# Weight loads for gating tied to evictions, and the last normalised rows written to other tiles

## The chip, the core and the metric

The kernel runs on one core of a Trainium2 chip. Its engines work side by side, each through its own queue in program order: PE (TensorE, matrix products into PSUM banks), DVE (VectorE) and ACT (ScalarE), which read PSUM and SBUF, POOL (GpSimd), which also issues DMAs, and SP (SyncE), which here only issues DMAs. Semaphores order them. The metric is the device time of one execution in microseconds (us); the median of several runs is compared.

## The reference

One layer of a diffusion backbone over 1024 latent tokens and 256 context tokens, model width 1024, everything in float32. Cut to what matters here:

```python
h_lat = rms_norm(x, norm1_g) * (1 + sc1) + sh1
p = h_lat @ w_in                      # 7 column blocks of 512: retention q,k,v,gate; attention q,k,v
y = concat(retention(...), diff_attention(...)) @ w_out
x = x + g1 * y                        # g1: one number for each of the 1024 columns
h2 = rms_norm(x, norm2_g) * (1 + sc2) + sh2
x = x + g2 * conv_ffn(h2, w_up, conv_w, conv_b, w_down)
return rms_norm(x, final_g)
```

The projection, the retention (chunks of 128 tokens, two directions), the attention, the output projection and the feed-forward part follow one another; every product of `rms_norm` needs a row's whole sum of squares first.

## The kernel before

**Products in halves.** Float32 operands are split into a high and a low part (`whi` on ACT, `wlo` on DVE) and each product is three passes on PE: high by high, high by low, low by high (lines 133 to 135). The two large products, the output projection and the feed-forward part, are built by a scheme of seven block products instead of eight, so that sums and differences of blocks are formed first (`sums_in_place`, `combined`, `t1_d`, `w13_d`, `w2_d`).

**The projection.** `stream_block(b)` loads one column block of `w_in` in four slices of 512 KB (`raw`, line 195, on SP) and splits each into `whi` and `wlo` (lines 202 and 203). There are two buffers for `raw` and five for the split slices, so a fifth slice, slice 0 of the next block, is split early and the others when PE has finished with the old block. `natural` then makes eight tiles of 128 tokens, `pn`, each of 24 matmuls; `store_to` evicts a tile on ACT (`st`, line 469) and stores it. At each of the eight steps of a tile `tick()` advances two side jobs by rates. In the block of the retention's gates (number 3) and the one of the attention's values (number 6) these are:

- `side`: with block 3 `states_before`, the backward states of the retention. It loads keys and values in pairs (`kvgb`, line 237, on SP, three pairs ahead), multiplies on PE (`pub`, line 363) and updates the state on DVE (`Sb`, lines 248 and 250). With block 6 it is `outputs`: 32 steps of scores, outputs, square root on POOL (line 119), gating of a head and transposing (`pc`, `po`, `ss`, `o`, `y`, `pyt`).
- `along`: `weight_blocks`, which multiplies `w_out` by g1. It loads the 1024 gate numbers (`g1`, 512 KB over 128 partitions, on SP) and, for c = 0 to 3, two blocks of `w_out` of 512 KB on POOL's DMA queue (`load`, line 423), multiplies their halves by g1 on DVE (`gated`, line 427), forms a difference (`t1`) and a combination on DVE, and stores three results on POOL's queue (`kept`, line 430). Its rate is 0.3 steps a tick, beginning at a count of −5. The loads themselves wait only for their buffers (an older tile's last reader); nothing ties them to a place in the projection.

**The output projection's end.** `out_product` makes a 512-wide half of 128 rows; `to_x1` adds it to `x1[t]` on DVE (line 1347). `squared` stores that half of `x1[t]` to DRAM for the last residual (`x1d`, line 1285, on SP) and sums its squares on ACT. `norm2` adds the two sums, takes the power −1/2 on POOL (line 1297) and scales the whole row block in place (line 1298). Rows 0 to 3 come first; rows 7, 4, 5, 6 are the last, in this order. In between stand `turned0` (rows 0 to 3 transposed and split into B11 and B21), the splitting of the first three weight blocks of the feed-forward part (`early`), and the sums of two further blocks, one on DVE and one on POOL (`sums_in_place`, lines 1329 to 1331; POOL goes on with `combined`, line 1512). Behind that PE begins the feed-forward products (`chain`, `second`) with `turned1` beside them: rows 4 to 7 transposed (`pt`, line 1304), combined on DVE (line 1454) and split. The products `fifth`, `third` and the later ones of `chain` follow.

**What sets the order.** Instructions are written in the order of the Python code, a scheduler orders each engine's queue by its own estimates, and `tc.issue_after` or `tc.add_manual_dep` ties one instruction to another. A dependency of class NoSync fixes the order alone; one of class Sync is a wait. Here the order of `weight_blocks` among its neighbours follows from the two numbers above.

Of the kernel before, what the change touches and what calls it, by code (L numbers as in the profile page):

```python
# [8 lines left out]
F32 = mybir.dt.float32  # L9
# [3 lines left out]
ALU = mybir.AluOpType  # L13
# [4 lines left out]
P = 128  # L18
D = 1024
# [40 lines left out]

TAIL = 2
GAP = 128
PREP_RATE, PREP_DUE = 0.3, -5.0
SPARE = (16, 4)
MOD_TICKS = 7
FIRST_LOADS = (22, 23, 25, 26, 28, 30)
# [10 lines left out]
def kernel(  # L77
# [16 lines left out]
    nc = tc.nc  # L94
# [17 lines left out]
    mhalf = kp.tile([P, 32], F32, name="mhalf")  # L112
# [27 lines left out]
    g1_d = dr.tile([P, D], F32, name="g1d")  # L140
# [19 lines left out]
    with ExitStack() as p1:  # L160
# [26 lines left out]
        marks = {}  # L187
# [227 lines left out]
        def weight_blocks():  # L415
            shared = rp.tile([P, 2, 2, 512], F32, name="g1", tag="rtab")
            g1 = shared[:, 0]
            nc.sync.dma_start(out=g1.rearrange("p n e -> p (n e)"), in_=g1_d)
            blocks = {}

            def load(c, i):
                t = blocks[c, i] = shared[:, 1] if c % 2 > i else er.tile([P, 2, 512], F32, name=f"w{i}x", tag="xhl")
                nc.gpsimd.dma_start(out=t, in_=w_out[:, :, 4 * i + c, :].rearrange("n p e -> p n e"))

            def gated(t, half):
                with tc.issue_after(marks["last"]):
                    nc.vector.tensor_tensor(out=t[:, half, :], in0=t[:, half, :], in1=g1[:, half, :], op=ALU.mult)

            def kept(dst, o):
                nc.gpsimd.dma_start(out=dst, in_=o)  # L430

            load(0, 0)
            load(0, 1)
            load(1, 0)
            for c in range(4):
                wa, wb = blocks[c, 0], blocks.get((c, 1))
                for half in range(2):
                    yield
                    gated(wa, half)
                    if c and not half:  # L440
                        load(c, 1)
                        wb = blocks[c, 1]
                yield
                t1 = er.tile([P, 512], F32, name="t1", tag=("xa", "xb")[c % 2])
                with tc.issue_after(marks["last"]):
                    nc.vector.tensor_tensor(out=t1, in0=wa[:, 1, :], in1=wa[:, 0, :], op=ALU.subtract)
                kept(t1_d[c], t1)
                for half in range(2):
                    yield
                    gated(wb, half)  # L450
                kept(w2_d[c], wb)
                yield
                nc.vector.tensor_tensor(out=wa[:, 1, :], in0=wb[:, 1, :], in1=wa[:, 1, :], op=ALU.subtract)
                kept(w13_d[c], wa)
                if c < 2:
                    load(c + 2, 0)

        def natural(wget, lhs, tiles, finish):
            for t in tiles:
# [6 lines left out]
        def store_to(dst, func=AF.Copy, scale=1.0, c0=0, center=False):  # L466
            def fin(t, pt):
                st = ev.tile([P, 4, P], F32, name="st", bufs=3)
                nc.scalar.activation(st.rearrange("p h e -> p (h e)"), pt, func, scale=scale)
                if center:  # L470
                    mu = ev.tile([P, 32], F32, name="mu")[:, 0:4]
                    nc.vector.tensor_reduce(out=mu, in_=st, axis=AX.X, op=ALU.add)
                    nc.vector.tensor_scalar(out=mu, in0=mu, scalar1=1.0 / P, scalar2=None, op0=ALU.mult)
                    nc.vector.tensor_tensor(out=st, in0=st, in1=mu.unsqueeze(2).to_broadcast([P, 4, P]), op=ALU.subtract)
                nc.sync.dma_start(out=dst(c0 + t), in_=st)

            return fin
# [815 lines left out]
    def norm2(t):  # L1293
        squared(t, right if t < 4 else left)
        rs = sm2[:, t : t + 1]
        nc.vector.tensor_tensor(out=rs, in0=rs, in1=sm2[:, NT + t : NT + t + 1], op=ALU.add)
        power = nc.gpsimd.tensor_tensor(out=rs, in0=rs, in1=mhalf[:, :1], op=ALU.pow).ins
        nc.vector.tensor_scalar(out=x1[t], in0=x1[t], scalar1=rs, scalar2=None, op0=ALU.mult)
        return power

    def turned(hf, d, raw, on_act):
        pt = turn_tile[0]()
# [30 lines left out]
    with ExitStack() as p3:  # L1333
# [10 lines left out]
                tick()  # L1344

        def to_x1(t, cols, ps):
            nc.vector.tensor_tensor(out=x1[t][:, cols], in0=ps, in1=x1[t][:, cols], op=ALU.add)

        def split_into(o, src):
            nc.scalar.copy(o[:, 0, :], src)  # L1350
# [74 lines left out]
            to_x1(4 + r, right, chain[r])  # L1425
            squared(4 + r, right)
        pre = [raw_load("wra" if j < 2 else "wrb", w_up[j]) for j in range(NPRE)]
        early = [[split_op(a[:, c : c + 4, :]) for c in (0, 4)] for a in pre]
        raws = [up_load(j) for j in range(NSUM)]
        sums_in_place(nc.vector, *raws[0])  # L1430
        for r in (3, 0, 1, 2):
            out_product(chain[r], r, y22o, t4o, False)
            to_x1(4 + r, left, chain[r])
            scaled = norm2(4 + r)
        with tc.issue_after(scaled):
            sums_in_place(nc.gpsimd, *raws[1])
        beside(iter(()), 0.0)
    x1lS.close()

# [79 lines left out]
        return dict(p1=a1, p2=a2, p3=b1, p4=b2, p5=s1, p6=s2, p7=s3)  # L1519

    chain, second, first, fifth, third = {}, {}, {}, {}, {}
    with tc.issue_after(scaled):
        ops = [combined(j) for j in range(NSUM)]
    split_ahead = []
    beside(turned1(), 0.5, -2.5)
    for j in range(NPRE):
# [522 lines left out]
```

## Time and profile before

| | |
|---|---|
| median of 3 runs | 1389.15 us (1388.04 to 1390.73) |
| the profiled execution | 1389.36 us |
| its span, first to last instruction | 1387.6 us |
| mean granted clock of TensorE | 0.996 |
| busy: PE, DVE, ACT, POOL | 1357.2, 1055.5, 758.5, 385.2 us |
| projection blocks 3 and 6 (latent tokens) | some 269 to 397 us of the span |
| last rows of the output projection | some 728 to 748 us |

All times in the profile are us from the first instruction. A row of the timeline has start, duration, engine, line, operation, written tile `<-` read tiles, shapes and a count; in square brackets stands how long the engine had been idle before it and what ended that. A row of waits has the waiting instruction, the one waited for, the sum, the number of waits and the longest. A row of stretches has the stretch, its length, the busy time of PE, PE's weight loads, DVE, ACT and POOL with the numbers of instructions, then the granted clock, the share of the 16 DMA engines that was busy, and GB/s. `SPq` rows are DMA issues. Line numbers are those of the kernel before.

### The profile page before, as it was taken

The numbers are of one execution on the slowest core, as the hardware profiler recorded it, in microseconds if no ns is written. First come the engines' busy times: TensorE is split into PE (matmuls) and PEld (weight loads), VectorE is DVE, ScalarE is ACT, GpSimd is POOL, SyncE is SP. The second block draws the span as 40 slices with busy tenths as digits, with TensorE's granted clock in tenths as the row PEclk, the third lists the DMA queues.
The fourth block names the chain that finished last, engine by engine and source line by source line (L and its number), as shares of the span: only waits on it lengthen the run. The fifth ranks groups of instructions, "written<-read, shape, count | busy, mean of one in ns | idle before, by whom it ended". The sixth has DMA issues, their size and how long they took to land.

```text
span 1387.6 us, 19752 instructions
## 1 busy us (share of the span) xinstructions
PE 1357.2 (98%) x6980; PEld 1138.4 (82%) x6980; DVE 1055.5 (76%) x1543; ACT 758.5 (55%) x1462; POOL 385.2 (28%) x422
## 2 busy tenths in 40 slices
PE   7999999999999999999999999999999999999997
PEld 5788888877888789999887888888888888788886
DVE  4967766644566888888878999888778877898756
ACT  5536534312457789988546645555544555455533
POOL 1310001611545354542102244222333220043003
PEclk9999999999999999999999999999999999999999
DMA  9467887799669595340714223332323326953324
GB/s 379 157 201 255 293 271 245 255 329 323 213 225 248 129 254 119 64 86 1 273 69 129 91 107 115 114 114 93 112 104 110 114 76 221 373 190 109 125 99 152
DMA packets 111499, 240.60 MB, mean 173 GB/s; under 512 B 10212, under 2 KB 42468, under 8 KB 109992
## 3 DMA queue, kind: packets, MB, share of 16 engines
q1 hardware_dynamic: 100360, 206.30, 43.7%
q0 software_dynamic: 10896, 32.77, 9.5%
q8 instruction: 55, 0.90, 0.3%
q14 instruction: 44, 0.36, 0.1%
q10 hardware_dynamic: 144, 0.26, 0.1%
HBM read 170.62 MB, written 68.42 MB: 172 GB/s over the span
## 4 chain that ended last, share of the span: by engine, by line
PE 61%; DMA 3%; DVE 1%; POOL 1%; issue 0%; ACT 0%; SPq 0%; POOLq 0%; DVEq 0%; ACTq 0%
PE chain L133 6%; PE chain L134 6%; PE chain L135 6%; PE pA L959 5%; PE pv L991 5%; PE c L135 4%; PE c L134 4%; PE c L133 4%; PE third L133 3%; PE third L135 3%; PE third L134 3%; PE pt L979 2%; DMA W<-w_down 2%; PE second L135 1%; PE second L134 1%; PE second L133 1%
## 5 line engine op out<-in xcount | busy, mean ns | idle before, releaser
L133 PE MATMUL pl<-hT,whi 128*128 128x512 f32 x256 | 107.6, 420 | 0.0
L133 PE MATMUL chain<-T,whi 128*128 128x512 f32 x264 | 102.8, 390 | 0.0
L134 PE MATMUL chain<-T,whi 128*128 128x512 f32 x264 | 102.7, 389 | 0.0
L135 PE MATMUL chain<-T,wlo 128*128 128x512 f32 x264 | 102.7, 389 | 0.0
L962 DVE TENSOR_REDUCE mt<-pA 128x1 f32<-128x1280 f32 x64 | 95.1, 1489 | 9.1 <-PE pA L959 8.4
L135 PE MATMUL pl<-hT,wlo 128*128 128x512 f32 x256 | 100.5, 392 | 0.0
L134 PE MATMUL pl<-hT,whi 128*128 128x512 f32 x256 | 100.2, 391 | 0.0
L1515 POOL TENSOR_TENSOR cmb<-wrb 128x512 f32<-128x512 f32 x20 | 30.5, 1523 | 235.1 <-DMA wrb<-w_up 171.3
L135 PE MATMUL c<-whi,ghl 128*128 128x512 f32 x232 | 90.4, 389 | 1.1 <-DVE ghl L1810 1.1
L134 PE MATMUL c<-wlo,ghl 128*128 128x512 f32 x232 | 90.3, 389 | 0.0
L133 PE MATMUL c<-whi,ghl 128*128 128x512 f32 x232 | 90.3, 389 | 0.0
L959 PE MATMUL pA<-ks,qhl 128*128 128x512 f32 (+1 forms) x384 | 89.6, 368 | 0.0
L966 ACT ACTIVATE p<-pA,mt 128x1280 f32<-128x1280 f32 x64 | 85.4, 1334 | 4.4 <-DVE mt L962 4.0
L133 PE MATMUL pn<-whi,hT 128*128 128x512 f32 x192 | 85.7, 446 | 1.2 <-ACT whi L202 1.2
L503 ACT ACTIVATE xb<-pl 32x512 f32<-32x512 f32 (+1 forms) x88 | 51.9, 590 | 60.9 <-PE pl L135 41.3
L1252 ACT CAST whi<-cmb 128x512 fp32r<-128x512 f32 x62 | 38.4, 622 | 77.1 <-PE chain L134 61.9
L135 PE MATMUL pn<-whi,hT 128*128 128x512 f32 x192 | 76.6, 400 | 1.0 <-POOL hT L668 1.0
L959 PEld LDWEIGHTS pA<-ks,qhl 128*128 128x128 f32 x384 | 68.1, 190 | 11.4
L134 PE MATMUL pn<-wlo,hT 128*128 128x512 f32 x192 | 76.2, 397 | 0.8 <-DVE wlo L203 0.8
L991 PE MATMUL pv<-va,aT 128*128 128x128 f32 x640 | 76.8, 275 | 0.0
L991 PEld LDWEIGHTS pv<-va,aT 128*128 128x128 f32 x640 | 74.0, 192 | 0.4 <-ACT aT L985 0.3
L1252 ACT CAST whi<-wra 128x512 fp32r<-128x512 f32 x55 | 33.7, 621 | 68.9 <-PE third L134 42.3
(428 smaller groups left out, 3989.7 us busy)
## 6 DMA issues: line engine op xcount, KB each, us to landing
raw<-w_in SPq DMA_DIRECT2D x32, 512.0 KB, 6.1
wm<-w_mod SPq DMA_DIRECT2D x32, 512.0 KB, 4.7
wra<-w_up SPq DMA_DIRECT2D x24, 512.0 KB, 3.4
wrb<-w_up SPq DMA_DIRECT2D x23, 512.0 KB, 3.5
W<-w_down SPq DMA_DIRECT2D x44, 256.0 KB, 5.8
ad<-s SPq DMA_DIRECT2D x20, 512.0 KB, 3.3
wra<-ad SPq DMA_DIRECT2D x20, 512.0 KB, 3.3
wrb<-ad SPq DMA_DIRECT2D x18, 512.0 KB, 3.7
```

The costliest lines, as they stand in the source:

```text
L133: mm(ps, lh, rh, start=first, stop=False, skip_group_check=more)
L134: mm(ps, lh, rl, start=False, stop=False, skip_group_check=more)
L135: mm(ps, ll, rh, start=False, stop=last, skip_group_check=more)
L503: nc.scalar.activation(xb[q * blk : (q + 1) * blk, :], pt[o : o + blk, :], AF.Copy, scale=scale)
L959: mm(self.pa[m][:, c0:c1], self.q[:, i, m, qs], self.k[:, m, c0:c1], start=(i == 0), stop=(i == 1))
L962: nc.vector.tensor_reduce(out=self.mt[:, m : m + 1], in_=self.pa[m][:, :LK], axis=AX.X, op=ALU.min)
L966: self.exp_ins = nc.scalar.activation(self.p[m], self.pa[m][:, :LK], AF.Exp, scale=-1.0, bias=self.mt[:, m : m + 1], accum_out=self.s[:, m ...
L979: nc.tensor.transpose(self.pt[g][:, i, :], self.p[0][:, (4 * g + i) * P : (4 * g + i + 1) * P], ident)
L991: mm(self.pv, self.aT[:, c, :], self.v[:, c, :], start=(c == 0), stop=(c == NKT - 1))
L1252: nc.scalar.copy(hi, src)
L1515: eng.tensor_tensor(out=s1, in0=b1, in1=b2, op=ALU.add)
```

## The change

```diff
-PREP_RATE, PREP_DUE = 0.3, -5.0
+PREP_RATE, PREP_DUE = 0.4, -5.8
...
             shared = rp.tile([P, 2, 2, 512], F32, name="g1", tag="rtab")
             g1 = shared[:, 0]
-            nc.sync.dma_start(out=g1.rearrange("p n e -> p (n e)"), in_=g1_d)
             blocks = {}
+            def behind(ins):
+                tc.add_manual_dep(ins, marks["pn"].name, mybir.DependencyInfo(mybir.DependencyClass.Sync, mybir.DependencyReason.DATA), reason="later")
-            def load(c, i):
+            def load(c, i, later=False):
                 t = blocks[c, i] = shared[:, 1] if c % 2 > i else er.tile([P, 2, 512], F32, name=f"w{i}x", tag="xhl")
-                nc.gpsimd.dma_start(out=t, in_=w_out[:, :, 4 * i + c, :].rearrange("n p e -> p n e"))
+                ins = nc.gpsimd.dma_start(out=t, in_=w_out[:, :, 4 * i + c, :].rearrange("n p e -> p n e")).ins
+                if later:
+                    behind(ins)
...
-            load(0, 0)
-            load(0, 1)
-            load(1, 0)
+            behind(nc.gpsimd.dma_start(out=g1.rearrange("p n e -> p (n e)"), in_=g1_d).ins)
+            load(0, 0, True)
+            load(0, 1, True)
+            yield
+            load(1, 0, True)
+            yield
             for c in range(4):
+                if c == 2:
+                    for _ in range(9):
+                        yield
+                    along["rate"] = 0.45
+                    load(2, 0, True)
+                    load(2, 1, True)
+                    yield
+                    load(3, 0, True)
+                    yield
...
-                    if c and not half:
+                    if c % 2 and not half:
                         load(c, 1)
...
-                if c < 2:
-                    load(c + 2, 0)
...
-                nc.scalar.activation(st.rearrange("p h e -> p (h e)"), pt, func, scale=scale)
+                marks["pn"] = nc.scalar.activation(st.rearrange("p h e -> p (h e)"), pt, func, scale=scale).ins
...
-        power = nc.gpsimd.tensor_tensor(out=rs, in0=rs, in1=mhalf[:, :1], op=ALU.pow).ins
-        nc.vector.tensor_scalar(out=x1[t], in0=x1[t], scalar1=rs, scalar2=None, op0=ALU.mult)
-        return power
+        nc.gpsimd.tensor_tensor(out=rs, in0=rs, in1=mhalf[:, :1], op=ALU.pow)
+        src = x1[t]
+        if t >= 4:
+            x1[t] = opp.tile([P, D], F32, name=f"xs{t}", tag=f"w{t - 4}")
+        return nc.vector.tensor_scalar(out=x1[t], in0=src, scalar1=rs, scalar2=None, op0=ALU.mult).ins
...
-        early = [[split_op(a[:, c : c + 4, :]) for c in (0, 4)] for a in pre]
+        early = [[split_op(a[:, c : c + 4, :]) for c in (0, 4)] for a in pre[:1]]
         raws = [up_load(j) for j in range(NSUM)]
-        sums_in_place(nc.vector, *raws[0])
         for r in (3, 0, 1, 2):
             out_product(chain[r], r, y22o, t4o, False)
-            to_x1(4 + r, left, chain[r])
+            added = to_x1(4 + r, left, chain[r])
+            if r != 3:
+                tc.add_manual_dep(scaled, added.name, mybir.DependencyInfo(mybir.DependencyClass.NoSync, mybir.DependencyReason.DATA), reason="order")
             scaled = norm2(4 + r)
-        with tc.issue_after(scaled):
-            sums_in_place(nc.gpsimd, *raws[1])
+        last_scaled = scaled
+        early += [[split_op(a[:, c : c + 4, :]) for c in (0, 4)] for a in pre[1:]]
+        sums_in_place(nc.vector, *raws[0])
+        ordered = len(nc.cur_bb.bb.instructions)
+        sums_in_place(nc.gpsimd, *raws[1])
...
-    with tc.issue_after(scaled):
-        ops = [combined(j) for j in range(NSUM)]
+    ops = [combined(j) for j in range(NSUM)]
+    for ins in nc.cur_bb.bb.instructions[ordered:]:
+        if ins.engine == mybir.EngineType.Pool:
+            tc.add_manual_dep(ins, last_scaled.name, mybir.DependencyInfo(mybir.DependencyClass.Sync, mybir.DependencyReason.DATA), reason="later")
```

`marks["pn"]` is the last eviction written so far. So the load of g1, now on POOL's queue, and the first three loads of `w_out` wait for the eviction of the second tile of block 3; the loads for c = 2 and the first for c = 3 wait for the eviction of the first tile of block 6. Between the work for c = 1 and that for c = 2 nine empty steps are put. The last four row blocks are scaled into the buffers of `w22o`, which are free by then; POOL's sums wait for the last of these scalings, where they stood behind the last power before.

The next rows are SP's queue in the first tiles of block 3 (`g` is the tile of g1, `raw` a slice of `w_in`, `kvgb` keys and values for the states), before:

```order
L418 DMA g_2701<-g1d 128x1024
L513 DMA rqk_78<-xa 128x4x128
L489 DMA rqk_78<-xq 128x4x256
L237 DMA kvgb<-kvg_79 128x512
L475 DMA kvg_80<-st 512x1x128
L195 DMA raw<-w_in 128x1024
L237 DMA kvgb<-kvg_83 128x512
L195 DMA raw<-w_in 128x1024
L237 DMA kvgb<-kvg_82 128x512
```

and now (numbers of lines are those of the changed file):

```order
L195 DMA raw<-w_in 128x1024
L527 DMA rqk_78<-xa 128x4x128
L503 DMA rqk_78<-xq 128x4x256
L237 DMA kvgb<-kvg_79 128x512
L489 DMA kvg_80<-st 512x1x128
L195 DMA raw<-w_in 128x1024
L237 DMA kvgb<-kvg_83 128x512
L195 DMA raw<-w_in 128x1024
L237 DMA kvgb<-kvg_82 128x512
```

The first `raw`, slice 0 of block 6, has moved up five places to where the load of g1 stood; slices 1 and 2 moved up by one load of `raw` each.

The next rows are POOL's queue where the blocks for c = 2 and 3 begin and the first outputs of the retention follow (`w0x`, `w1x`, `g` are blocks of `w_out`; `t1d`, `w2d`, `w13d` the stores; `ss` a power, `y` a head's gated output), before:

```order
L423 DMA w1x<-w_out 128x2x512
L423 DMA g_2701<-w_out 128x2x512
L430 DMA t1d_146<-t_3044 128x512
L430 DMA w2d_154<-w1x 128x1024
L430 DMA w13d_150<-w0x 128x1024
L423 DMA w1x<-w_out 128x2x512
L119 TENSOR_TENSOR ss<-ss,mhalf 128x2
L312 TENSOR_TENSOR y<-o 128x128
```

and now:

```order
L425 DMA w0x<-w_out 128x2x512
L425 DMA w1x<-w_out 128x2x512
L425 DMA g_2679<-w_out 128x2x512
L119 TENSOR_TENSOR ss<-ss,mhalf 128x2
L434 DMA t1d_146<-t_3166 128x512
L312 TENSOR_TENSOR y<-o 128x128
L313 TENSOR_TENSOR y<-y,kvgf 128x128
L119 TENSOR_TENSOR ss<-ss,mhalf 128x2
```

The stores for c = 2 stood ahead of the first power and now stand among the outputs, with the load of the second block for c = 3 behind them.

The last rows are DVE's queue around the last additions (`x_4` to `x_7` are the row blocks, `xs` the new tiles, `sm` the sums and powers, `B` low parts of transposed rows 0 to 3, `wra`, `wrb` weights of the feed-forward part), before:

```order
L1347 TENSOR_TENSOR x_4_7057<-oc_7100,x_4_7057 128x512
L1312 TENSOR_TENSOR B_7571<-raw_7061,B_7571 128x512
L1347 TENSOR_TENSOR x_5_7058<-oc_7101,x_5_7058 128x512
L1298 TENSOR_SCALAR x_7_7060<-x_7_7060,sm_7062 128x1024
L1296 TENSOR_TENSOR sm_7062<-sm_7062 128x1
L1347 TENSOR_TENSOR x_6_7059<-oc_7102,x_6_7059 128x512
L1298 TENSOR_SCALAR x_4_7057<-x_4_7057,sm_7062 128x1024
L1296 TENSOR_TENSOR sm_7062<-sm_7062 128x1 x2
L1298 TENSOR_SCALAR x_5_7058<-x_5_7058,sm_7062 128x1024
L1298 TENSOR_SCALAR x_6_7059<-x_6_7059,sm_7062 128x1024
```

and now:

```order
L1363 TENSOR_TENSOR x_5_7058<-oc_7101,x_5_7058 128x512
L1315 TENSOR_SCALAR xs_7764<-x_4_7057,sm_7062 128x1024
L1267 TENSOR_TENSOR wlo<-wrb,whi 128x512
L1310 TENSOR_TENSOR sm_7062<-sm_7062 128x1
L1345 TENSOR_TENSOR wrb<-wrb 128x512
L1363 TENSOR_TENSOR x_6_7059<-oc_7102,x_6_7059 128x512
L1315 TENSOR_SCALAR xs_7784<-x_5_7058,sm_7062 128x1024
L1346 TENSOR_TENSOR wra<-wrb,wra 128x512
L1310 TENSOR_TENSOR sm_7062<-sm_7062 128x1
L1347 TENSOR_TENSOR wra<-wra 128x512
L1315 TENSOR_SCALAR xs_7804<-x_6_7059,sm_7062 128x1024
```

Each row block is now added one place ahead of the scaling of its neighbour, and the splits and sums of the weights (`wlo`, `wrb`, `wra`), which stood ahead of the additions, stand between them. The set of operations up to the last scaling is the same.

More of the change, by code (lines that the diff above doesn't have):

```diff
@@ L1346, in to_x1 @@
         def to_x1(t, cols, ps):
-            nc.vector.tensor_tensor(out=x1[t][:, cols], in0=ps, in1=x1[t][:, cols], op=ALU.add)
+            return nc.vector.tensor_tensor(out=x1[t][:, cols], in0=ps, in1=x1[t][:, cols], op=ALU.add).ins
         def split_into(o, src):
```

## The prediction

> **What bounds the kernel now.** I read the page's busy line first, then the list of PE's waits, then the clock by stretches, and last the timelines around the two largest waits.
>
> ```profile
> PE 1357.2 (98%) x6980; PEld 1138.4 (82%) x6980; DVE 1055.5 (76%) x1543; ACT 758.5 (55%) x1462; POOL 385.2 (28%) x422
> PE pub L363 <- DVE Sb L250: 2.8, 1, 2.8
> PE pt L1304 <- DVE x L1298: 2.5, 2, 1.3
> PE pn L133 <- ACT whi L202: 1.2, 1, 1.2
> PE pn L134 <- DVE wlo L203: 0.8, 1, 0.8
> 282.00:292.00 10.00, 7.16 (x37) 5.72 (x36) 2.96 (x8) 2.12 (x3) 0.72 (x1) 1.00 1.02 369
> 332.30:335.70 3.40, 3.40 (x10) 2.62 (x9) 3.03 (x4) 0.60 (x1) 1.13 (x2) 0.52 0.99 402
> 748.60:752.10 3.50, 3.50 (x13) 2.84 (x12) 3.44 (x4) 1.39 (x2) 3.42 (x3) 0.53 0.00 0
> ```
>
> TensorE is the bound: 98% busy, so only what it waits for, or runs slowly through, can be won. In the rows of stretches the last three numbers are granted clock, DMA share and GB/s. PE waits 2.84 us near 287, 1.18 + 0.76 near 330 and 2.50 near 746, and behind the second and the third of these the clock is halved: 3.4 us at 0.52 cost 1.6, 3.5 us at 0.53 cost 1.6. Both parts of the change aim at these places; together they hold 4.78 + 1.6 = 6.4 us (stage A, the gating) and 2.50 + 1.6 = 4.1 us (stage B, the last rows).
>
> **Stage A, what is removed.** The next rows are from the timelines of ACT, DVE, SP, POOL and from the stretches.
>
> ```profile
> 286.84 1.04 ACT L202 CAST whi<-raw 128x1024 fp32r<-128x1024 f32 x1 [11.31 <-DMA raw<-w_in]
> 287.92 1.23 DVE L203 TENSOR_TENSOR wlo<-raw,whi 128x1024 fp32r<-128x1024 f32 x1 [5.74 <-ACT whi L202]
> 272.53 0.38 SPq L418 DMA_DIRECT2D g<-g1d  x1
> 278.07 1.86 SPq L195 DMA_DIRECT2D raw<-w_in  x1
> 272.43 0.97 POOL L423 DMA_DIRECT2D g<-w_out  x1 [3.16 <-DVE xb L507]
> 275.90 0.76 POOL L423 DMA_DIRECT2D w0x<-w_out  x1
> 284.76 0.72 POOL L423 DMA_DIRECT2D w1x<-w_out  x1 [8.11 <-DMA rqk<-xq]
> 270.00:282.00 12.00, 12.00 (x60) 10.10 (x59) 4.19 (x10) 2.61 (x4) 4.20 (x4) 1.00 0.98 331
> raw<-w_in SPq DMA_DIRECT2D x7, 512.0 KB, 5.8
> ```
>
> The first wait is a chain: slice 0 of the next block's weights (raw, issued at 278.07) lands only at 286.8; ACT's cast waits for it, DVE's low part waits for the cast, the state updates queue behind that on DVE, and PE runs out of buffers for `pub`. In those microseconds the DMA engines are full (share 0.98, then 1.02), and 2 MB of them are the four gating loads of 512 KB. The change does two things. The four loads wait for the eviction of the second projection tile, whose place on ACT is behind that very cast, so they cannot start before slice 0 is in. And slice 0 takes the place of the gate's load in SP's queue: 272.5 instead of 278.1. With the median 5.8 us it lands at 278.3. DVE comes to its low part at about 278; it was held there 5.74 + 1.15 us and PE paid 2.84 of it, so 4.05 us are free, and a landing up to about 279.8 costs PE nothing. **The 2.84 us go**, with 1.5 us to spare.
>
> ```profile
> 319.53 0.56 POOL L430 DMA_DIRECT2D w2d<-w1x  x1 [3.62 <-DVE w1x L427]
> 320.26 0.54 POOL L430 DMA_DIRECT2D w13d<-g  x1 [0.17 <-DVE Sb L250]
> 322.01 2.26 SPq L195 DMA_DIRECT2D raw<-w_in  x2
> 325.47 0.72 POOL L423 DMA_DIRECT2D w1x<-w_out  x1 [4.67 <-DMA w2d<-w1x]
> 318.00:332.00 14.00, 12.06 (x58) 9.56 (x57) 8.59 (x14) 5.38 (x6) 2.56 (x4) 1.00 1.01 342
> 329.13 1.04 ACT L202 CAST whi<-raw 128x1024 fp32r<-128x1024 f32 x1 [3.75 <-DMA raw<-w_in]
> ```
>
> The second wait is slice 3 of that block: issued at 322.01, landed at 329.1, 7.1 us, with two stores and a load of 512 KB each around it at a share of 1.01. In the change block 1 of the gating is stored 9 ticks of the projection earlier (counted by the rates its last store is due at tick 52 and not 61; a projection tile has 8 ticks), and blocks 2 and 3 are asked for only in tick 75 and after, behind the next projection's first eviction. So 1.5 MB leave the stretch; at 342 GB/s that is 4.4 us of transfers. Not all of it stood before slice 3: I take the two stores, 1 MB or 3 us, and the slice lands 4.1 us after its issue. PE needed it 1.94 us sooner: **1.18 + 0.76 and the half clock behind it, 1.6, go as well.**
>
> **Stage A, what is added.** Nothing is computed more; six more DVE operations of 0.69 us and three 512 KB loads move into the next projection, where the retention's outputs run beside it. Block 3 stands there already, and PE is busy 10.00 of 10 us beside it.
>
> ```profile
> 340.00:350.00 10.00, 10.00 (x63) 8.83 (x62) 5.04 (x15) 3.56 (x12) 3.21 (x5) 1.00 0.61 195
> 397.90 0.30 PE L317 MATMUL pyt<-ident,y 128*128 128x128 f32 x1 [0.33 <-POOL y L312]
> DMA to landing us min/median/max: 4.4/6.6/8.6
> ```
>
> The added wait has a queue on POOL: behind a held gating DMA there stand the powers and y products of the outputs, for which DVE and then PE's `pyt` wait. Lower bound 0 (PE had no wait there with half this work); upper bound 2.84, if a gating product on DVE meets a block that has not landed and holds the state updates again: landing takes 4.4 to 8.6 us, and the products come 7 to 8 ticks behind the issue. I take one wait near the 0.33 above, 0.4, the nearest row. **Stage A: 6.4 − 0.4 = 6.0 us.**
>
> **Stage B.** The rows are DVE's, POOL's, SP's and PE's.
>
> ```profile
> 730.75 1.28 DVE L1253 TENSOR_TENSOR wlo<-wra,whi 128x512 fp32r<-128x512 f32 x2
> 742.92 0.75 DVE L1298 TENSOR_SCALAR x<-x,sm 128x1024 f32<-128x1024 f32 x1 [1.03 <-issue]
> 743.65 0.68 DVE L1347 TENSOR_TENSOR x<-oc,x 128x512 f32<-128x512 f32 x1
> 745.88 2.42 DVE L1298 TENSOR_SCALAR x<-x,sm 128x1024 f32<-128x1024 f32 x2 [0.53 <-POOL sm L1297]
> 748.23 1.76 DVE L1253 TENSOR_TENSOR wlo<-wrb,whi 128x512 fp32r<-128x512 f32 x1
> 746.33 1.42 POOL L1329 TENSOR_TENSOR wrb<-wrb 128x512 f32<-128x512 f32 x1
> 740.24 0.39 PE L135 MATMUL oc<-t4o,y22o 128*128 128x512 f32 x1
> 745.23 0.31 PE L1304 MATMUL pt<-ident,x 128*128 128x128 f32 x1
> 748.36 0.44 PE L1304 MATMUL pt<-ident,x 128*128 128x128 f32 x2 [1.34 <-DVE x L1298]
> ```
>
> PE has the last row's product at 740.6, but DVE adds it at 743.65: the scaling of row 7 at 742.92 stood before it and waited, with no engine named, for the store that still read the tile it overwrites. The last two scalings took 1.21 us each beside POOL's sums (0.75 without), and ended at 748.30; PE wanted them at 745.23. The change scales into other tiles, so no store is waited for, puts each addition before the neighbour's scaling, and holds POOL's sums behind the last one. The same operations stand before that last scaling, in another order: from 730.75 these are sixteen 512-wide ones at 0.605 from start to start, one eviction of 0.72, four scalings of 0.67, four small sums of 0.08: 13.4 us. With some 1.2 us for the weights' landing (which held a cast 1.39 us) and the last power, the last scaling ends at 745.3: 3.0 us earlier. PE then waits about 0.2 instead of 2.50, and the half clock has no cause: PE is 2.3 + 1.6 = 3.9 us ahead.
>
> What is late next is DVE, which is only 3.0 us ahead.
>
> ```profile
> 790.00:800.00 10.00, 10.00 (x45) 8.11 (x44) 9.90 (x8) 7.64 (x13) 8.02 (x5) 1.00 0.16 52
> 794.69 1.28 DVE L1253 TENSOR_TENSOR wlo<-cmb,whi 128x512 fp32r<-128x512 f32 x2
> 795.47 0.45 PE L135 MATMUL third<-T,wlo 128*128 128x512 f32 x1
> 795.76 0.40 PE L133 MATMUL third<-T,whi 128*128 128x512 f32 x1
> ```
>
> DVE is 9.90 of 10 us busy here. At 795.47 a matmul takes `wlo` 0.1 us after DVE made it, and the next starts 0.29 later instead of 0.23: no slack is left there. So PE's lead at 795 is what DVE's is. DVE loses some of its 3.0 again, because all 8 us of POOL's sums now stand against its own work and not 6; of some 1.1 us lost per operation (1.76 against 0.68) I count half of one. Bounds: 1.8 (one whole operation lost) and 3.9 (no loss, other slack found). **Stage B: 2.4 us**, with a new wait of 1.5 near 795.
>
> **Sum.** The profiled execution took 1389.36 (its span 1387.6 and 1.8 around it). 6.0 + 2.4 = 8.4 gives 1380.96; the median of the three runs is 0.21 below that execution, so **1380.8**, its own range 1378.9 to 1382.
>
> **The rivals**, from the median 1389.15.
> 1. *DVE does not hold PE near 795*, and the gating costs nothing: 6.4 + 3.9 = 10.3, **1378.8**. For it: DVE's waits on ACT may shrink. Against: the 0.1 us at 795.
> 2. *A late landing takes one stall's place*: slice 0 after 279.8, or a gating block behind its product. It gives 2.84 back: 8.4 − 2.8, **1383.6**. For it: margins of 1 to 2 us beside landings that scatter over 4 us.
> 3. *The wait near 795 halves the clock*: 8.4 − 1.6, **1382.4**. 1.94 and 2.50 us of idling did it, 1.5 is just under.
> 4. *The half clock is not caused by these waits* and stays: 6.0 and 2.4 lose 1.6 in stage A; in B PE's 2.3 is below DVE's lead, so 0.1: 8.4 − 1.7, **1382.4**. In the rows the half clock follows two of the three waits within 2 us and the 2.84 us one not at all, which speaks a little for it; that it stands nowhere else inside the program speaks against. [...]
> 5. *The change does not do what it says*: the bytes are the same and the transfers late as before, DVE gives stage B back: about 0, **1389.1**. Against: the order shows slice 0 moved five places up in SP's queue.
> 6. *Slower*: slice 2's load now stands three places behind slice 1's, ahead of state loads, and SP waits there until slice 0 is split. If slice 0 lands at 286.8 as now, SP stands still from 280.5 to 289.1, 8.6 us; the state loads (median 4.4 us, three pairs ahead) come some 7 us late and PE waits that long, with two half clocks (3.2) and the old 2.84: 13 against 8.4, **1393.8**. It decides where slice 0 lands later than some 284.
>
> ```profile
> kvgb<-kvg SPq DMA_DIRECT2D x20, 256.0 KB, 4.4
> ```
>
> **How the numbers follow.** Forecast 0.46, rival 1 0.14, rival 2 0.18, rival 3 0.06, rival 4 0.03, rival 5 0.07, rival 6 0.06. Faster by over 0.2% (2.8 us, about what a measurement of this kernel can tell from no change): the first five cases, 0.87; within: 0.07; slower: 0.06. The range takes in the forecast's own and rivals 1 to 4, with 0.5 us at the lower end and 1 at the upper for their spread: 1378.3 to 1384.6.
>
> **What would show it.** Right: the cast of slice 0 near 279 and none of the four waits left; clock 1.00 from 300 to 760; the last scaling ending 3 us sooner after its stage's first matmul; a new PE wait on `wlo` near 790 (8 us earlier in the span) of 1 to 2 us. Wrong: PE waiting on `Sb` or `pc` behind a gating product, a cast of `raw` waiting over 3 us, or `pt` still waiting for its scaled rows.

## The result, and the profile after

The changed kernel takes **1380.63 us** in the median of four runs, the kernel before 1389.37 beside it. One of the four ran at a granted clock of 0.65 and took 1938.45; the other three (1379.09 to 1381.12) have a median of 1380.14, and the ratio is of these: 0.9933, with an interval of 0.9914 to 0.9953. The forecast was 1380.8. The profiled execution took 1381.12 us, its span 1379.3.

The first rows are the page's busy line, three rows of TensorE's list of waits and five of the table of stretches.

```profile
PE 1355.3 (98%) x6980; PEld 1137.3 (82%) x6980; DVE 1054.1 (76%) x1543; ACT 758.6 (55%) x1462; POOL 388.7 (28%) x423
PE pt L1320 <- ACT r L1322: 1.7, 2, 0.9
PE pyt L317 <- POOL y L313: 1.5, 1, 1.5
PE pn L134 <- DVE wlo L203: 0.7, 1, 0.7
280.00:290.00 10.00, 10.00 (x53) 8.47 (x52) 3.66 (x9) 1.82 (x3) 2.96 (x4) 1.00 1.06 391
322.00:332.00 10.00, 10.00 (x47) 8.05 (x46) 3.31 (x5) 3.30 (x4) 2.15 (x3) 1.00 0.87 258
735.00:745.00 10.00, 10.00 (x53) 8.28 (x52) 8.77 (x12) 4.63 (x8) 7.19 (x6) 1.00 0.38 116
745.00:755.00 10.00, 8.28 (x46) 6.40 (x44) 9.83 (x14) 8.03 (x14) 2.36 (x2) 1.00 0.00 1
25.50:29.00 3.50, 3.50 (x10) 2.58 (x9) 1.92 (x5) 2.10 (x5) 0.00 (x0) 0.51 1.02 425
```

`pub` no longer waits for `Sb`, and TensorE is busy throughout 280 to 290 and 322 to 332. The half clocks near 332 and 749 are gone. Two things are not as the prediction had them. `pt` still waits 1.7 us, now for ACT's evictions and no longer for the scaled rows. And a half clock stands at 25.5, in code that the change does not touch.

To see where the time went I set the same matmul of both traces side by side and take the difference of their starts, the changed kernel's lead. It is −1.36 us at 265 of the old span (the start's half clock, and a 0.67 us wait near 167), 5.99 at 420, 5.99 at 700, 8.12 at 830 and 8.30 at 1340. So stage A won 7.35 in this execution and stage B 2.13, and 1.36 was lost before either. Each lead at a time, here and below, is the median over the matmuls of 5 us.

Stage A in the changed kernel, from the timelines of ACT, DVE, SP and POOL:

```profile
273.89 0.38 SPq L195 DMA_DIRECT2D raw<-w_in  x1
279.86 1.05 ACT L202 CAST whi<-raw 128x1024 fp32r<-128x1024 f32 x1 [2.97 <-DMA raw<-w_in]
280.94 1.23 DVE L203 TENSOR_TENSOR wlo<-raw,whi 128x1024 fp32r<-128x1024 f32 x1 [1.55 <-ACT whi L202]
283.92 0.79 POOL L436 DMA_DIRECT2D g<-g1d  x1 [7.03 <-ACT st L483]
320.26 2.26 SPq L195 DMA_DIRECT2D raw<-w_in  x2
325.07 1.05 ACT L202 CAST whi<-raw 128x1024 fp32r<-128x1024 f32 x1 [1.45 <-DMA raw<-w_in]
```

Slice 0 is cast at 279.86, 6.0 us after its issue, and the gating loads start at 283.92, behind the eviction. Slice 3 is cast 4.8 us after its issue; it was 7.1. With the 1.36 us that this execution is behind at that point, the cast stands at 278.5 of the old span: the prediction had the landing at 278.3 and a margin to 279.8. TensorE did not wait.

Stage B, from the timelines of DVE, POOL, ACT and PE:

```profile
738.52 0.75 DVE L1315 TENSOR_SCALAR xs<-x,sm 128x1024 f32<-128x1024 f32 x1 [0.44 <-POOL sm L1311]
742.24 1.74 POOL L1346 TENSOR_TENSOR wra<-wrb,wra 128x512 f32<-128x512 f32 x1
742.75 1.77 DVE L1267 TENSOR_TENSOR wlo<-wrb,whi 128x512 fp32r<-128x512 f32 x1
744.45 1.77 DVE L1474 TENSOR_TENSOR raw<-r,raw 128x512 f32<-128x512 f32 x1
746.25 0.62 ACT L1327 CAST T<-raw 128x512 fp32r<-128x512 f32 x1 [2.77 <-DVE raw L1474]
746.78 0.77 ACT L1322 ACTIVATE r<-pt,m 128x512 f32<-128x512 f32 x1
747.61 0.65 PE L1320 MATMUL pt<-ident,xs 128*128 128x128 f32 x4 [0.88 <-ACT r L1322]
750.50 0.66 PE L1320 MATMUL pt<-ident,xs 128*128 128x128 f32 x4 [0.84 <-ACT r L1322]
```

The last scaling ends at 739.27. With it the old waits are gone, for the scaled rows and behind them the half clock: against the kernel before, TensorE's lead in stage B rises to 4.56 near 752 of the old span. It does not keep it. By 765 the lead is 2.39. Read the rows as a chain: two DVE operations beside POOL's sums take 1.70 from start to start, not 0.605. So ACT stands 2.77 us idle ahead of a cast of `raw`, the eviction behind that cast is late, and `pt` waits until it is done.

The last rows of this stage are the place near 795 of the old span where the prediction saw DVE hold TensorE:

```profile
786.52 1.28 DVE L1267 TENSOR_TENSOR wlo<-cmb,whi 128x512 fp32r<-128x512 f32 x2
786.92 0.39 PE L134 MATMUL third<-T,whi 128*128 128x512 f32 x1
787.25 0.50 PE L135 MATMUL third<-T,wlo 128*128 128x512 f32 x1
787.60 0.40 PE L133 MATMUL third<-T,whi 128*128 128x512 f32 x1
```

The first of the two low parts ends at 787.20. The matmul that takes it starts 0.05 later, and 0.33 and not 0.23 behind the one ahead of it. Over this place the lead falls by another 0.20.

### The profile page after: what moved, and what is told of

It reads as the page before. It is cut to its first block, busy times and chain, and to the rows that moved or that the text cites. A ratio compares the mean times of both kernels' runs of the same rounds, so it can differ in the third digit from the quotient of the medians.

```text
span 1379.3 us, 19755 instructions
## 1 busy us (share of the span) xinstructions
PE 1355.3 (98%) x6980; PEld 1137.3 (82%) x6980; DVE 1054.1 (76%) x1543; ACT 758.6 (55%) x1462; POOL 388.7 (28%) x423
## 4 chain that ended last, share of the span: by engine, by line
PE 62%; DMA 2%; DVE 1%; POOL 1%; ACT 1%; issue 0%; SPq 0%; POOLq 0%; DVEq 0%; ACTq 0%
PE chain L133 6%; PE chain L134 6%; PE chain L135 6%; PE pA L973 5%; PE pv L1005 5%; PE c L135 4%; PE c L134 4%; PE c L133 4%; PE third L135 3%; PE third L133 3%; PE third L134 3%; PE pt L993 2%; DMA W<-w_down 2%; PE second L134 1%; PE second L133 1%; PE second L135 1%
```

## The experiments

Every kernel was run with a profile, 5 to 12 times, beside the kernel before, in three groups; the latter's median was 1388.37 in the first (`a_alone` to `a_sp`), 1389.47 in the second (`a_nopause` to `b_alldve`) and 1387.56 in the third. So kernels of different groups are compared by their ratios.

### The halves apart

`a_alone` has the diff's part up to `store_to`; of the rest it has what stood there before:

```diff
-            x1[t] = opp.tile([P, D], F32, name=f"xs{t}", tag=f"w{t - 4}")
...
-                tc.add_manual_dep(scaled, added.name, ...)
...
+        with tc.issue_after(scaled):
+            sums_in_place(nc.gpsimd, *raws[1])
```

> Only the gating half of the change; the last rows are scaled, added and summed as in the kernel before. Theory (the two halves add, each through TensorE's own waits): the waits for the state update (2.84 us) and for raw slice 3 (1.18 + 0.76) are gone and so is the half clock behind the second, the old wait of 0.33 near 398 stays gone; pt still waits 2.5 us for scaled rows with a half clock behind it. 6.5 to 7.2 us below the kernel before: 1382.2 to 1382.9, ratio 0.995. Rival 1 (the 7.2 us seen in the changed kernel hold something that the other half brought): 6.0 or less, 1383.4. Rival 2 (the shift in time alone puts the 2.5 us of pt's wait across two clock windows): 1.6 better, 1381.

1382.22 us, ratio 0.9952 (0.9940 to 0.9964). The lead won in stage A is 5.47. The ratio is the theory's 0.995, but two waits that it had as gone are in the profile: slice 3 still held TensorE up 0.22 and 0.77, and `pyt` waited 0.37 near 392. The profile also did what rival 2 says: `pt` waited 1.05 and 1.34 and no half clock followed; a boundary of the 3.41 us grid of the last section lies between the two (at 740.9).

`b_alone` is the kernel before with the complement:

```diff
+            x1[t] = opp.tile([P, D], F32, name=f"xs{t}", tag=f"w{t - 4}")
...
+                tc.add_manual_dep(scaled, added.name, ...)
...
-        with tc.issue_after(scaled):
-            sums_in_place(nc.gpsimd, *raws[1])
```

> Only the last-rows half of the change; the gating is loaded as in the kernel before. Theory (DVE's chain is the bound there: what the scalings win, 3 us, DVE loses partly beside POOL's sums, and PE meets it at the turns of the last rows or at the low parts some 45 us later): pt waits some 1.7 us in place of 2.5, no half clock behind it, 2.4 us below the kernel before: 1387.0, ratio 0.9983. Rival 1 (DVE holds nothing, the 1.7 us came from how the two halves meet): 3.9 below, 1385.5. Rival 2 (the clock stays halved because it follows a fixed grid and not these waits): 0.8 below, 1388.6.

1386.15 us, ratio 0.9988 (0.9979 to 0.9998): between 0.3 and 2.9 us, the theory's 2.4 within, but rival 2's 0.8 as well. The profile is against rival 2: `pt` waits 1.02 and 0.83 with no half clock behind, and the lead won in stage B is 2.0. So `pt`'s new waits do not come from how the halves meet. The two ratios multiply to 0.9940; the whole has 0.9933, so the halves add within their intervals.

### Stage A: place, hold or pause

`a_free`: no load is held.

```diff
             def behind(ins):
-                tc.add_manual_dep(ins, marks["pn"].name, ...)
+                pass
```

> The changed kernel, but the four gating loads are not held for the eviction of the second projection tile: they start as soon as POOL comes to them, near 277, 3 us after slice 0 of the next weights. Slice 0 keeps its early place on SP. Theory P (the place in SP's queue carries the gain): slice 0 issued 273.9 lands before 281, PE waits under 0.5 us, 1380.6 to 1381. Theory H (holding the 2 MB carries it): slices 0 to 2 share the full DMA engines with 2 MB, slice 0 or 1 lands 2 to 3 us later than in the changed kernel, PE waits 1 to 2.8 us near 280 to 288: 1381.6 to 1383.5.

1386.34 us, ratio 0.9985 (0.9975 to 0.9995): worse than either theory. The edit freed more than the text above says: the three loads for c = 2 and 3 too, and these decide. ACT, POOL, SP and PE:

```profile
279.86 1.05 ACT L202 CAST whi<-raw 128x1024 fp32r<-128x1024 f32 x1 [4.33 <-DMA raw<-w_in]
318.00 0.72 POOL L425 DMA_DIRECT2D w1x<-w_out  x1 [2.88 <-DMA w2d<-w1x]
319.20 0.74 POOL L425 DMA_DIRECT2D g<-w_out  x1 [0.48 <-DMA w13d<-g]
320.53 1.38 SPq L195 DMA_DIRECT2D raw<-w_in  x2
327.82 1.04 ACT L202 CAST whi<-raw 128x1024 fp32r<-128x1024 f32 x1 [5.18 <-DMA raw<-w_in]
328.92 0.79 PE L133 MATMUL pn<-whi,hT 128*128 128x512 f32 x1 [2.60 <-ACT whi L202]
```

For the first stall theory P holds: slice 0, at its early place, is cast at 279.86 with three of the four loads (1.5 MB) issued before it landed, and TensorE does not wait. The second stall is back, and larger: two loads of 512 KB start just ahead of slice 3, which lands 7.3 us after its issue; TensorE waits 2.60 and 0.47, and two windows of half clock follow (granted clock 0.51 from 328.5 to 335.4).

`a_sp`: the gate's load back on SP, unheld; the weights' loads stay held.

```diff
-            behind(nc.gpsimd.dma_start(out=g1.rearrange("p n e -> p (n e)"), in_=g1_d).ins)
+            nc.sync.dma_start(out=g1.rearrange("p n e -> p (n e)"), in_=g1_d)
```

> The changed kernel, but the gate's own load stands on SP's queue as before, unheld and ahead of slice 0, which so keeps its old late place (issued near 278); the three weight loads stay held. Theory H (holding carries the gain): with 0.5 MB beside it and not 2 MB, slice 0 lands at 283.9 or sooner, PE waits under 0.5 us there, 1380.6 to 1381.2. Theory P (the place carries it): it lands near 286 as before, the state updates queue behind the cast and PE waits 2 to 2.8 us for them: 1382.6 to 1383.5.

1380.73 us, ratio 0.9942 (0.9930 to 0.9954). From SP and ACT:

```profile
275.82 0.71 SPq L195 DMA_DIRECT2D raw<-w_in  x1
282.48 1.05 ACT L202 CAST whi<-raw 128x1024 fp32r<-128x1024 f32 x1 [8.66 <-DMA raw<-w_in]
```

Slice 0 is cast at 282.48, 2.6 us later in the span than in the changed kernel and 5.7 later in the program (the lead at 265 is 1.71 here and −1.36 there), and still TensorE waits only 0.19 for `Sb`. So either edit alone removes the first stall, but for this 0.19.

`a_nopause`: the first loads held, no pause and no hold for c = 2 and 3.

```diff
-                if c == 2:
-                    for _ in range(9):
-                        yield
-                    along["rate"] = 0.45
-                    load(2, 0, True)
...
+                if c < 2:
+                    load(c + 2, 0)
```

> The changed kernel without the pause: blocks 2 and 3 of the output weights are asked for as soon as block 0 and 1 are stored (as before the change), at the higher rate 0.4. The first loads stay held. Theory (1.5 MB of stores and loads around raw slice 3 made it late): two or three transfers of 512 KB stand beside slices 2 and 3 again, slice 3 lands 2 us later than in the changed kernel, PE waits 1 to 2 us near 324 with a half clock behind it: 1382 to 1384.2. Rival (the higher rate alone moves block 1's stores out of the way): no wait near 324, 1380.6.

1389.48 us, ratio 1.0002 (0.9992 to 1.0011): the whole gain of the change is gone, more than the theory expected, and by another road. POOL, DVE and PE:

```profile
318.31 0.72 POOL L425 DMA_DIRECT2D w1x<-w_out  x1 [4.38 <-DMA w2d<-w1x]
325.66 0.69 DVE L431 TENSOR_TENSOR w1x<-w1x,g 128x512 f32<-128x512 f32 x1 [6.50 <-DMA w1x<-w_out]
327.54 0.80 PE L134 MATMUL pn<-wlo,hT 128*128 128x512 f32 x1 [3.57 <-DVE wlo L203]
```

A gating product stands on DVE ahead of a slice's low part. DVE is idle for 6.50 us until its block lands; the low part behind it is ready at 327.5, and TensorE has waited 3.57 us. This is the mechanism that the prediction named as the upper bound of what stage A adds; the hold and the pause of c = 2 and 3 are what keeps it away. Over the stage the lead falls by 0.90, where the changed kernel wins 7.35.

### Stage B: tiles, order and hold

Four kernels take away the tiles, the hold, both, and the order.

```diff
 b_inplace, b_orderonly
-        if t >= 4:
-            x1[t] = opp.tile([P, D], F32, name=f"xs{t}", tag=f"w{t - 4}")
 b_poolfree, b_orderonly
-    for ins in nc.cur_bb.bb.instructions[ordered:]:
-        if ins.engine == mybir.EngineType.Pool:
-            tc.add_manual_dep(ins, last_scaled.name, ...)
 b_noorder
-            if r != 3:
-                tc.add_manual_dep(scaled, added.name, ...)
...
-        early += [[split_op(a[:, c : c + 4, :]) for c in (0, 4)] for a in pre[1:]]
-        sums_in_place(nc.vector, *raws[0])
```

(In `b_noorder` all of `early` and DVE's three sums stand ahead of the rows again.)

> The changed kernel with the last four rows scaled in place, not into other tiles; the order on DVE and the hold of POOL's sums stay. Theory (the wait for the store that reads the tile is a part of what made the rows late): each scaling waits for the store of the row's unscaled form to land (4 to 5 us after its issue), the last scaling ends 3 us or more later than in the changed kernel, pt waits over 2 us more and the clock is halved behind it: 1384 to 1386. Rival (order and hold alone make the rows early): 1380.6.

> The changed kernel without the hold of POOL's sums; one of them (of the other weights) then stands ahead of the last power on POOL, the rest behind it. Theory (POOL's sums cost DVE about 1.1 us for each DVE operation beside them wherever they stand, so the hold only chooses which operations pay): the last power and scaling come 1 to 1.5 us later, but 1.3 us of sums are out of the way sooner: 1380.2 to 1381.4. Rival (the hold carries the gain of the last rows): 2 us later, pt waits in one window long enough to halve the clock, 1382.6 to 1384.2.

> The changed kernel with the last rows scaled in place and POOL's sums not held: of the second half only the order is left (each addition ahead of the neighbour's scaling; the later weights' splits and DVE's sums behind the rows). Theory (the order alone carries the second half, the tile is worth the 0.7 us that a scaling waits for the store and the hold nothing): 0.3 to 1 us above the changed kernel, 1380.8 to 1381.8. Rival (tile or hold is needed, each covers for the other's absence): as with the first half alone or worse, 1382.5 to 1384.

> The changed kernel with other tiles and held sums, but in the old order: the later weights' splits and DVE's three sums stand ahead of the last rows, and no addition is tied ahead of a scaling. Theory (the order carries the second half): the last scaling ends 2 to 3 us later than in the changed kernel, pt waits 2 to 2.5 us, in one window with a half clock: 1382.2 to 1384. Rival (the tiles carry it, since an addition can pass a scaling that overwrites nothing): 1380.6 to 1381.

| kernel | last product to end of last scaling, us | `pt`'s waits, us | lead won in stage B, us | median, us | ratio |
|---|---|---|---|---|---|
| `a_alone` (none) | 7.93 | 1.05, 1.34, 0.77 | −0.05 | 1382.22 | 0.9952 (0.9940 to 0.9964) |
| `b_noorder` (tiles, hold) | 6.55 | 1.15, 0.97, 0.85 | 0.47 | 1382.41 | 0.9960 (0.9948 to 0.9973) |
| `b_orderonly` (order) | 8.15 | 2.84 | 0.63 | 1382.08 | 0.9959 (0.9947 to 0.9972) |
| `b_inplace` (order, hold) | 6.58 | 1.26, 0.95, 0.84 | 0.49 | 1381.24 | 0.9939 (0.9927 to 0.9951) |
| `b_poolfree` (tiles, order) | 6.07 | 0.75, 0.77, 0.15 | 1.94 | 1380.36 | 0.9933 (0.9921 to 0.9946) |
| changed kernel (all) | 5.01 | 0.88, 0.84 | 2.13 | 1380.63 | 0.9933 (0.9914 to 0.9953) |
| changed kernel, again | 4.81 | 0.88, 0.84 | 1.91 | 1380.66 | 0.9950 (0.9938 to 0.9963) |

The second column runs from the start of the last matmul of `oc` to the end of the last row's scaling; the kernel before has 8.06. The leads are against the kernel before, which has a half clock in this stage; none of these has one. That by itself won nothing: `a_alone` lost the half clock, was 1.72 ahead near 752 of the old span, and gave all of it back, to `pt`'s next waits and at the low part near 795. Each lead is of one execution. Stage B's full code stands in three more profiles without a half clock there and won 2.00 (`b_alone`), 1.54 (`a_free`) and 1.17 (`a_nopause`). So by the traces **tiles and order are needed together**: either without the other wins 0.5 to 0.6, both win 1.2 to 2.1, and the hold shows no gain once they are there. `b_poolfree` came as its theory said, in time and in the last scaling (1.06 later). For `b_inplace` the theory was too dear. DVE's rows show what in-place scaling pays:

```profile
731.77 0.75 DVE L1313 TENSOR_SCALAR x<-x,sm 128x1024 f32<-128x1024 f32 x1 [0.78 <-DMA x1d<-x]
739.30 0.75 DVE L1313 TENSOR_SCALAR x<-x,sm 128x1024 f32<-128x1024 f32 x1 [1.04 <-DMA x1d<-x]
```

It waits 0.78 and 1.04 for stores, not 3. `b_noorder` took the time of its theory, but its last scaling came 1.5 later, not 2 to 3, and `pt`'s waits brought no half clock. `b_orderonly` lies between its theory and its rival; its last scaling is as late as in the kernel before, so there the rival is nearer. The ratios agree with the traces but cannot rank the kernels by themselves: the changed kernel's own two, 0.9933 and 0.9950, differ by more than that of `b_inplace` from the first.

### POOL's sums on DVE

```diff
-        sums_in_place(nc.gpsimd, *raws[1])
+        sums_in_place(nc.vector, *raws[1])
...
-    ON_VECTOR = 0
+    ON_VECTOR = 2
```

> The changed kernel with POOL's five sums (7.8 us on POOL) done by DVE instead, right after the last scaling: 5 x 0.605 = 3.0 us more on DVE, and the 4.1 us that DVE lost beside them (four operations of 1.5 to 1.7 us from start to start, not 0.605) go. Theory (DVE's chain bounds PE from the last rows to the low parts near 787, and POOL's sums slow DVE): DVE is 1.1 us or more ahead after them, and 1.2 us of its idle time near 739 is filled; pt's two waits of 0.9 and 0.8 us shrink: 1379.0 to 1380. Rival 1 (pt's waits come from ACT's evictions, not from DVE): no change, 1380.6. Rival 2 (three sums now stand ahead of the low parts that PE takes first): a new wait of 1 to 2 us near 741, 1381.6 to 1382.6.

1379.60 us, ratio 0.9929 (0.9915 to 0.9942). The next rows are stretches, PE's timeline and, near 785, DVE's and PE's:

```profile
735.00:745.00 10.00, 10.00 (x54) 8.31 (x53) 9.15 (x16) 4.80 (x9) 0.98 (x1) 1.00 0.25 77
745.00:755.00 10.00, 9.59 (x50) 7.42 (x49) 9.62 (x16) 9.88 (x18) 0.00 (x0) 1.00 0.00 1
746.07 0.66 PE L1320 MATMUL pt<-ident,xs 128*128 128x128 f32 x4 [0.27 <-ACT r L1322]
784.29 1.28 DVE L1267 TENSOR_TENSOR wlo<-cmb,whi 128x512 fp32r<-128x512 f32 x2
785.02 0.51 PE L135 MATMUL third<-T,wlo 128*128 128x512 f32 x1
```

With POOL quiet, DVE does 32 operations in these 20 us and not 26. The waits of 0.88 and 0.84 shrink to 0.27 and 0.14, and the lead won in stage B is 3.50. DVE's own lead, taken at the low part near 795 of the old span, is 3.49 there; it was 2.18 in the changed kernel. That is 1.3 more, where the sums cost 4.1 beside POOL and 3.0 on DVE. ACT's evictions are as many as before, so rival 1 falls; no new wait near 741 appears, so rival 2 does too.

> The changed kernel once more, unedited, as the yardstick of these runs and for a second look at the halved clock: 1380.0 to 1381.2. Theory (the clock is halved where TensorE idles about 1.4 us or more within one window of a fixed 3.413 us grid that starts anew in each run): pt's two waits of 0.8 to 1 us fall into two windows, or into one, and then 1.6 us are lost; the start of the program is halved in some runs and not in others. Rival (the halved window near 25 us belongs to the changed kernel): it is there again.

The changed kernel, run again without an edit, takes 1380.66 us (1379.87 to 1381.38), ratio 0.9950 (0.9938 to 0.9963). The window near 25 is at full clock this time, after a wait of 1.32 that a boundary cut into 0.89 and 0.43, so the rival falls: it does not belong to the change. `pt`'s two waits fell into two windows. Leads: 0.76 at 265, then 6.95 won in stage A and 1.91 in B.

> The kernel with the five sums on DVE once more, beside the changed kernel on the same chip. Theory (POOL's sums slow DVE, which holds up ACT's and TensorE's turns of the last rows): 1.0 us below the changed kernel (1.7 us of pt's waits less some 0.5 that returns at the end), ratio to the kernel before 0.992 to 0.993. Rival (the 1 us of the first time was chance): within 0.3 us of the changed kernel.

1378.98 us, ratio 0.9937 (0.9923 to 0.9951), 1.7 us below the changed kernel beside it, where the theory had 1.0; the ratio is a little above its 0.992 to 0.993. `pt` waits 0.66 and 0.14, the lead won in stage B is 3.07. It is ahead both times, by 0.0004 and 0.0013 in the ratio. The intervals overlap with the changed kernel's, so the time alone does not settle it; the trace shows the mechanism both times. Its two medians are the lowest of this study.

## Why the prediction was right, step by step

**Stage A, removed: right.** Forecast 6.4 less 0.4; the nine profiles that hold the whole half show 5.29 to 7.35, 6.4 in the mean. The first stall went whole. Of the second, nothing was left in the changed kernel's two profiles, but 0.21 to 1.04 us of its 1.94 in the other seven; the half clock behind it went in all nine. The reading of the cause was half complete. Slice 0's place on SP and the hold were taken as one step, and each would have done. For the second stall the weight lies on c = 2 and 3: held and paused, the stage wins 5.3 to 7.4; paused but not held (`a_free`) 0.45; neither (`a_nopause`) −0.90. The prediction reckoned "4.4 us of transfers" there and did not see that undoing this step costs more than the stall of before.

**Stage A, added: wrong by 0.4, in size.** In the changed kernel's two profiles no new wait came, and of the old one of 0.33 near 398 at most 0.11 was left. It is no rule: in five of the other seven profiles with this code it stands at 0.19 to 0.48.

**Stage B, the last scaling: right.** It was to end 3.0 us sooner; from the last product it is 5.01 against 8.06.

**Stage B, "PE then waits about 0.2 instead of 2.50": the step that failed.** No wait for scaled rows is left, and TensorE's lead rises to 4.56, more than the 3.9 forecast. But then `pt` waits 1.72 for ACT's evictions, which the prediction had nowhere, and the lead falls to 2.39. What holds ACT up is DVE beside POOL's sums: `b_alldve` takes POOL away, and the waits shrink to 0.41.

**Stage B, "DVE loses some of its 3.0 again": right in kind, somewhat small in size.** Counted from the stage's start, DVE is 3.04 ahead at the end of the last scaling and 2.17 ahead from 763 of the old span on. It loses 0.87; half an operation of 1.1 was forecast. Beside POOL's sums it loses far more, four times some 1.1: from 741.26 on three operations take 1.49 to 1.70 from start to start and a pair 2.29, not 0.605 each, 4.1 us more together. But the kernel before lost some 4.5 beside the same sums (five operations of 0.95 to 1.83), so little of it is new.

**Stage B, "PE's lead at 795 is what DVE's is": right; "a new wait of 1.5 near 795": wrong in place and size.** In twelve of the thirteen profiles TensorE's lead won in stage B equals DVE's at that low part to within 0.05: 2.13 and 2.18 in the changed kernel, −0.05 and −0.04 in `a_alone`, 0.49 and 0.53 in `b_inplace`, 3.50 and 3.49 in `b_alldve`. In all twelve the matmul starts 0.05 or 0.06 us behind its low part, and the lead falls there, by 0.16 to 0.52. (In `a_sp` a half clock held TensorE itself back.) So DVE does hold TensorE, and `b_alldve`, which changes only who does the sums, moves both. But most of what TensorE is ahead it gives back some 40 us earlier, at the evictions: 2.17 there and 0.20 near 795, where the prediction had nothing and 1.5. **The total came out, 2.13 against 2.4, because DVE's lead sets it; where TensorE pays was missed.**

**The half clock: right that waits cause it, but a matter of luck as well.** The 1.6 us of stage B went in the changed kernel, and went in `a_alone` too, where `pt` still waits 2.39 for the rows. The last section shows why. In `a_alone` the stage won nothing by it (−0.05), so the 1.6 is no gain of its own where DVE sets the lead. Rival 4 is refuted for this kernel; the wait of 2.84, which spoke for it, was cut into 1.41 and 1.43 by a window's end.

**The sum.** 7.35 + 2.13, less the 1.36 lost at the start, plus 0.18 behind stage B is 8.30 of span, against 8.4 forecast. That it is so close owes something to chance: the unchanged first 265 us differ by up to 3.1 us from one execution to the next (leads of −1.36 to 1.71 in thirteen profiles), more than most single terms.

**The other rivals.** 1 (no holding near 795, the gating free) was right about the gating in the changed kernel's two profiles, but DVE does set TensorE's lead in stage B. 2 and 6 need a late slice 0, and it landed in time. 3 did not occur. 5 is refuted by both stages.

## What to carry to other kernels

When a load makes a queue of small work late, tie the competing loads to an event behind it, and do so for every load that can run ahead to the next such place: here the hold of the later loads was worth more than that of the first ones. Compare the leads of both engines and not only the waits: TensorE was 4.56 us ahead for a moment, and what remained was DVE's 2.18, given back at another place than the one where the two met before. And where one engine's work slows another's, as POOL's sums slowed DVE here, price the work of the helper by what the other loses: five sums on POOL cost DVE 4.1 us, and DVE does them itself in 3.0.

## What the runs showed of the hardware

**The half clock followed a fixed grid.** In each of the fourteen profiles the half clock came in pieces of 3.41 us, and within one execution their starts differed by whole multiples of 3.413 (in the kernel before, 332.40 and 748.83 are 122 apart; in the changed kernel 25.54 and the one behind the last product, 1373.80, are 395 apart). Dividing each trace by its own grid and adding up TensorE's idle time in each window, from 26 us on to the last products: of the windows at full clock, all 50 with 0.9 to 1.73 us of idling were followed by full clock, and all six with 1.94 to 2.50 by half clock. (The expectation's 1.4, close to the 1.37 ahead of 25.5 in the changed kernel, was too low.) Where TensorE stops at the program's end, windows with 1.90 (`b_inplace`) and 1.92 us (`a_alone`) were still followed by full clock and those with 2.12 and more by half (2.75 in the changed kernel). So among these windows the most idling with full clock behind it is 1.92 us and the least with half clock 1.94. A matmul's end is modelled, so these are not exact. The same wait of 1.95 us shows both. In `a_sp` it fell into one window, in `a_free` a boundary cut it at 755.24:

```profile
748.20:751.60 3.40, 1.45 (x9) 1.25 (x9) 3.23 (x7) 2.62 (x5) 0.00 (x0) 1.00 0.00 0
751.60:755.00 3.40, 3.40 (x11) 2.73 (x11) 3.40 (x6) 3.37 (x6) 0.00 (x0) 0.50 0.01 2
751.80:755.20 3.40, 2.64 (x13) 1.59 (x11) 3.40 (x4) 1.69 (x4) 2.06 (x2) 1.00 0.00 0
755.20:758.60 3.40, 2.20 (x13) 1.90 (x14) 3.23 (x6) 3.32 (x6) 0.00 (x0) 1.00 0.00 0
284.60:288.00 3.40, 2.02 (x10) 1.35 (x8) 0.08 (x1) 1.16 (x2) 0.72 (x1) 1.00 1.04 412
288.00:291.40 3.40, 1.94 (x11) 1.68 (x12) 2.30 (x5) 0.38 (x1) 0.00 (x0) 1.00 1.02 336
```

The first two rows are `a_sp`, the next two `a_free`. The last two are the kernel before, where a boundary near 288.0 cut the wait of 2.84 into 1.41 and 1.43. So the wait of 1.95 us was followed by 3.4 us at 0.50, which cost 1.7 more, or by nothing, by where in the grid it fell, and the grid lay elsewhere from profile to profile: boundaries at 332.40 in the kernel before, 25.54 in the changed one, 755.24 in `a_free` and 740.9 in `a_alone` are 1.31, 1.64, 0.89 and 0.21 us more than whole multiples of 3.413. In windows that were themselves halved less idling had a second one behind it: 0.81 us in `a_free` and 1.20 in `a_nopause`. The window ahead of 25.5 in the changed kernel, 1.37 us idle beside matmuls only 2 columns wide, was followed by half clock too, and 1.28 at that place in `b_alldve_again` was not; whether the narrow matmuls are the reason, no run shows.

**POOL and DVE.** Beside POOL's sums of 1.3 to 1.7 us DVE made about one operation for each of POOL's, if that one read SBUF alone: in the changed kernel those at 742.75, 744.45 and 746.14 took 1.69 or 1.70 from start to start, beside POOL's sums at 742.24, 744.05 and 745.63, where `b_alldve` with POOL quiet has 0.60 (742.80 to 743.39). The addition that reads a product from PSUM (`ua<-second,ua`) was not slowed: 0.60 or 0.61 from start to start in all twelve profiles in which POOL does the sums. In the rows of stage B 742.24 to 743.98 on POOL lies beside 742.75 to 744.52 on DVE. Why the one slows the other, no run here shows.
